# A decoder layer in seven-product matmuls: which quads take seven products where the left operand is new, when its sums are made, and the queues of the first loads

## The chip, the cores and the metric

The kernel runs on 1 core of a Trainium2 chip. The metric is the device time of one execution in microseconds (us); lower is better. The engines are PE (TensorE, matmuls), DVE (VectorE), ACT (ScalarE), POOL (GpSimd) and SP (SyncE, which here only issues DMAs). All inputs lie in HBM.

## The reference, cut to what matters

One layer on x of 256 tokens by 4096 features, in float32:

```python
def reference(x, norm_gain, w_in, conv_w, w_out, rel_bias, final_gain):
    ...
    u = rmsnorm(h, norm_gain[l])
    proj = jnp.einsum('bsd,df->bsf', u, w_in[l])          # 4096 -> 16384
    q, k, v, z_a, hc, b_gate, c_gate, z_c = jnp.split(proj, split_at, axis=-1)
    ...
    attn = moba_attention(q, k, v, rel_bias).reshape(B, S, ATTN_W) * jax.nn.silu(z_a)
    conv = b_gate * short_conv(c_gate * hc, conv_w[l]) * jax.nn.silu(z_c)
    mixed = jnp.concatenate([attn, conv], axis=-1)
    h = h + jnp.einsum('bsf,fd->bsd', mixed, w_out[l])    # 4096 -> 4096
    return rmsnorm(h, final_gain)
```

With 256 tokens there is one attention block, so attention is causal softmax over 256 positions with a bias by distance, for 16 heads of 128. The convolution has three taps. Nearly all the work is in the two projections.

## The kernel before

**Parts.** A float32 product is made of three matmuls. Each operand is split into hi (rounded to the fast type, on ACT) and lo (the rest, on DVE), and hi x hi, lo x hi and hi x lo are added up in PSUM (L533 to L535). A matmul takes a 128 x 128 block of the left operand as weights and 512 columns of the right one.

**Pairs and quads.** A pair `p` is two column blocks of 512 over all 4096 rows: 16 pairs of the input projection (0 to 15, ordered by `PAIRS`) and 4 of the output projection (16 to 19). A pair has 16 quads, each for one `q`: 256 rows of the contraction, so 2 token halves x 2 row blocks on the left and 2 x 2 blocks on the right. The list `ORDERS` says in which order a pair takes its quads; places are counted from 0. `load` fetches the 1 MB of weights of a quad (`raw`, three buffers), two quads ahead.

**Eight or seven products.** Written out, a quad is eight block products, 24 matmuls, into four PSUM banks (3, 8, 2, 4). A quad of the set `SEVEN` (q = 0, 2, 4, 6, 8, 10, 12) takes seven, 21 matmuls, by sums of blocks on both sides: DVE makes four sums of weight blocks (`sum`, L465 to L467) and splits seven blocks of them in place of four; the left operand needs sums too (`sums_of`, L112, four subtractions or additions of 128 columns, then `parts` on seven blocks). The products go to banks 1, 5, 6, 7 besides. I call such quads sevens and the others eights. When the last seven of a pair is through, `early` (or `out_early` in the output) reads banks 1, 5, 6 and 7 into four tiles `e` on DVE, and ACT scales them by the tokens' norm (L587); when the pair is through, `two_done` (or `out_end`) reads banks 3, 2, 4, 8 on DVE and adds them (late sums). In between `tasks_of` puts the attention or the convolution of an earlier pair, counted by block products after the last seven (`behind`).

**What sets the order.** A unit is one split of hi and lo: an eight has two, a seven three. `split` runs two units ahead of the matmuls, and hi and lo have a ring of three buffers, so ACT and DVE can be two units ahead of PE at most. The engines take their instructions in the order in which the scheduler has put them; an instruction that waits holds back those behind it on its engine. All DMAs stand in SP's queue in order.

**Where the left operand is new.** In pair 0 the x blocks are loaded quad by quad (`x_load`, 256 KB), scaled by the norm's gain and split (`x_parts`): for an eight straight into hi (L138) and lo (L139), for a seven by way of a tile `c` (L130), its sums (L114) and `parts` (L117, L118). The tiles `k` are kept for all 16 pairs. The sums of squares of x are made by ACT on eight further loads of 512 KB (`squares`). In pairs 15 and 16 the same is done with the mixed rows (`m_load` from a DRAM tile `m_d`, then `m_parts`), at the places in `M_AT`. Pair 0 takes the order `FIRST` and pair 16 `OUT_FIRST`, both with eights between sevens; the last seven stands at place 14 of pair 0, 13 of pair 16 and 12 of all others. All pairs have the same seven sevens.

**Start and end.** Eight matmuls on zeros (`WARM`) run ahead of the first quad. The first loads are x, the gains and the weights, all from SP. In the last pair the products of the last three units for banks 3 and 2 (the second token half) are kept back, `out_end` and `finish` of the first half are written ahead of them, and then the kept products run unit by unit, bank 3 and bank 2 in turn.

## Time and profile before

| | us |
|---|---|
| median of 3 runs | 1749.53 (1748.86 to 1749.96) |
| the profiled execution, whole | 1750.47 |
| its span, first to last instruction | 1748.4 |
| PE busy | 1715.6 |
| DVE busy | 1533.4 |
| ACT busy | 1035.3 |

The span is 2.1 us short of the execution's own time. Busy time of PE is the union of overlapping records: a matmul's record lasts about 0.39 us, while the next one starts 0.23 us after it, so a stage is judged by how many matmuls it got through. A window row gives, for each engine, busy us and the number of instructions that lie in it (x...), then the granted TensorE clock as a share of 2.4 GHz, the share of DMA time and GB/s. A record on a window's edge is counted on both sides.

### The profile page before, as it was taken

To read this page: it belongs to the slowest core of one execution; us is meant where nothing else is said; L and a number is where in the kernel's file an instruction comes from. 1 tells how busy PE (TensorE), PEld (TensorE's weight loads), DVE (VectorE), ACT (ScalarE), POOL (GpSimd) and SP (SyncE) were. 2 spreads that over 40 slices of the span, in tenths; PEclk is the share of its full clock that TensorE was granted. 3 is DMA by queue.
4 is the path that set the end of the run, shared out by engine and by line. 5 is a ranking of instruction groups with operands and counts; after the bars stand their busy time and mean duration, and the time that the engine had idled before them with its cause. 6 is when DMAs were issued, how large, how long until landed. Compare 5 with 4: busy or idle time off the path is not lost.

```text
span 1748.4 us, 20772 instructions
## 1 busy us (share of the span) xinstructions
PE 1715.6 (98%) x7638; PEld 1402.8 (80%) x7638; DVE 1533.4 (88%) x1678; ACT 1035.3 (59%) x1125; POOL 0.7 (0%) x6
## 2 busy tenths in 40 slices
...
GB/s 298 310 169 215 187 216 200 198 187 216 203 195 187 217 204 193 192 203 197 213 198 212 205 211 198 199 210 218 203 205 223 233 282 239 200 207 208 200 220 154
DMA packets 65265, 368.18 MB, mean 211 GB/s; under 512 B 8811, under 2 KB 13452, under 8 KB 24460
## 3 DMA queue, kind: packets, MB, share of 16 engines
...
HBM read 357.66 MB, written 9.18 MB: 210 GB/s over the span
## 4 chain that ended last, share of the span: by engine, by line
PE 90%; DVE 7%; issue 1%; ACT 1%; DMA 0%; SPq 0%; DVEq 0%; ACTq 0%
PE p L535 29%; PE p L533 29%; PE p L534 29%; DVE lo L477 3%; ACT hi L476 1%; DVE sum L465 1%; DVE sum L466 1%; DVE k L118 0%; DVE sum L467 0%; PE p L220 0%; PE p L227 0%; DVE c L114 0%; PE p L244 0%; DVE hg L400 0%; DVE hg L406 0%
## 5 line engine op out<-in xcount | busy, mean ns | idle before, releaser
L533 PE MATMUL p<-hi,k 128*128 128x512 f32 x2420 | 949.5, 394 | 14.0 <-ACT hi L476 11.3
L534 PE MATMUL p<-hi,k 128*128 128x512 f32 x2420 | 945.2, 391 | 0.5 <-DVE k L118 0.3
L535 PE MATMUL p<-lo,k 128*128 128x512 f32 x2420 | 930.8, 392 | 2.5 <-DVE lo L477 2.3
L477 DVE TENSOR_TENSOR lo<-raw,hi 128x1024 fp32r<-128x1024 f32 (+2 forms) x504 | 675.9, 1359 | 42.4 <-ACT hi L476 41.2
L476 ACT CAST hi<-raw 128x1024 fp32r<-128x1024 f32 (+2 forms) x504 | 581.6, 1165 | 209.0 <-PE p L534 173.1
L476 ACT CAST hi<-sum 128x1024 fp32r<-128x1024 f32 x280 | 295.0, 1053 | 444.5 <-PE p L534 244.8
L533 PEld LDWEIGHTS p<-hi,k 128*128 128x128 f32 x2420 | 455.1, 188 | 115.4 <-ACT hi L476 19.2
L535 PEld LDWEIGHTS p<-lo,k 128*128 128x128 f32 x2420 | 455.0, 188 | 106.9 <-DVE lo L477 10.0
L534 PEld LDWEIGHTS p<-hi,k 128*128 128x128 f32 x2420 | 456.4, 189 | 93.9 <-DVE k L118 3.1
L477 DVE TENSOR_TENSOR lo<-sum,hi 128x1024 fp32r<-128x1024 f32 x280 | 341.9, 1221 | 135.3 <-ACT hi L476 135.1
L465 DVE TENSOR_TENSOR sum<-raw 128x1024 f32<-128x1024 f32 x140 | 170.9, 1221 | 8.6 <-DMA raw<-in_w_dram 6.3
L467 DVE TENSOR_TENSOR sum<-sum,raw 128x512 f32<-128x512 f32 x140 | 95.9, 685 | 0.2
L466 DVE TENSOR_TENSOR sum<-sum,raw 128x512 f32<-128x512 f32 x140 | 95.8, 684 | 0.2
L587 ACT ACTIVATE e<-e,rT 128x512 f32<-128x512 f32 x56 | 37.8, 716 | 0.7 <-DVE e L320 0.7
L117 ACT CAST k<-c 128x896 fp32r<-128x896 f32 (+1 forms) x23 | 18.7, 813 | 9.8 <-PE p L535 7.7
L118 DVE TENSOR_TENSOR k<-c,k 128x896 fp32r<-128x896 f32 (+1 forms) x23 | 21.2, 927 | 1.5 <-ACT k L117 1.5
L258 DVE SCALAR_TENSOR_TENSOR am<-p,st,z 128x128 f32<-128x128 f32 x32 | 9.7, 344 | 7.5 <-PE p L255 7.5
L305 DVE SCALAR_TENSOR_TENSOR y<-p,cw,y 128x255 f32<-128x255 f32 (+1 forms) x32 | 15.2, 477 | 0.1
L114 DVE TENSOR_TENSOR c<-c 128x128 f32<-128x128 f32 x56 | 14.3, 282 | 0.1
L235 ACT ACTIVATE lg<-lg,st 128x256 f32<-128x256 f32 (+1 forms) x32 | 14.3, 447 | 0.0
L303 ACT ACTIVATE y<-p,cw 128x256 f32<-128x256 f32 x16 | 7.6, 473 | 11.2 <-PE p L301 11.2
L402 ACT ACTIVATE e<-hg 128x512 f32<-128x512 f32 x16 | 10.0, 625 | 6.9 <-DVE hg L400 6.6
...
## 6 DMA issues: line engine op xcount, KB each, us to landing
raw<-in_w_dram SPq DMA_DIRECT2D x254, 1024.0 KB, 4.8
raw<-in_wout_dram SPq DMA_DIRECT2D x64, 1024.0 KB, 4.8
...
hg<-in_xres_dram SPq DMA_DIRECT2D x4, 1024.0 KB, 9.5
...
```

The costliest lines, as they stand in the source:

```text
L117: nc.scalar.copy(dst[:, :, 0], c)
L118: nc.vector.tensor_tensor(dst[:, :, 1], c, dst[:, :, 0].bitcast(F32), ALU.subtract)
L305: nc.vector.scalar_tensor_tensor(y[:, i:], ps[:, :S - i], cw[:, k, 2 - i:3 - i], y[:, i:], op0=ALU.mult, op1=ALU.add)
L465: nc.vector.tensor_tensor(t[:, :2], raw[:, 1:3], raw[:, :1].to_broadcast([P, 2, B]), ALU.add)
L466: nc.vector.tensor_tensor(t[:, 2], t[:, 0], raw[:, 2], ALU.add)
L467: nc.vector.tensor_tensor(t[:, 3], t[:, 2], raw[:, 3], ALU.add)
L476: nc.scalar.copy(hi[:, c], src[:, c])
L477: nc.vector.tensor_tensor(lo[:, c], src[:, c], hi[:, c].bitcast(F32), ALU.subtract)
L533: nc.tensor.matmul(acc[b_], a, h_, start=s0, stop=False)
L534: nc.tensor.matmul(acc[b_], b, h_, start=False, stop=False)
L535: nc.tensor.matmul(acc[b_], a, l_, start=False, stop=s1)
L587: nc.scalar.activation(es[name], es[name], AF.Copy, scale=rows[c][:, t:t + 1])
```

## The change

- Pair 0 and pair 16 now have three sevens (q = 8, 10, 12) and 13 eights; pair 1 has five sevens (4 to 12 even). The set of sevens is kept for each pair (`SEVENS`). Both pairs take one new order `FIRST`, with the sevens at places 9, 11 and 13.
- The missing sums of q = 0, 2, 4, 6 are made later (`made_up`): the x blocks are loaded again and scaled in pair 1 after places 1 (q = 4), 3 (6), 12 (0) and 14 (2); the mixed rows are loaded again in pair 16 after places 6, 8, 10 and 12 (`RAISE`). The load is written one place ahead. The sum that stood in slot 7 of a left operand now replaces the block in slot 0.
- `M_AT` is a table, the operands of the mixed rows being spread over 16 places of pairs 15 and 16.
- The four scalings after `early` are put behind 5, 8, 11 and 14 block products, in all pairs of the input projection.
- The gains and the first x are loaded from ACT's queue, the first weights from SP's. There are 12 warm-up matmuls.
- At the end, the kept products of bank 3 all run ahead of those of bank 2, and `out_end` of bank 3 is written between them.

The diff:

```diff
--- before.py
+++ after.py
@@ -28,7 +28,7 @@
 QUAD = 4 * B
-WARM = 8
+WARM = 12
 AHEAD = 2
@@ -47,14 +47,24 @@
 SEVEN = frozenset((0, 2, 4, 6, 8, 10, 12))
-FIRST = (1, 3, 0, 5, 2, 7, 4, 9, 6, 11, 8, 13, 10, 14, 12, 15)
+FIRST = (1, 3, 5, 7, 0, 9, 2, 11, 4, 8, 6, 10, 13, 12, 14, 15)
 USUAL = (0, 1, 2, 3, 4, 5, 6, 7, 8, 9, 10, 11, 12, 13, 14, 15)
-OUT_FIRST = (1, 3, 5, 0, 7, 2, 9, 4, 11, 6, 13, 8, 12, 10, 14, 15)
 N_PAIRS = 16
...
 PAIRS += [x for g in range(4) for x in (((4, 6), g), ((7, 5), g))]
-ORDERS = [FIRST] + [USUAL] * (N_PAIRS - 1) + [OUT_FIRST] + [USUAL] * (NDP - 1)
+ORDERS = [FIRST] + [USUAL] * (N_PAIRS - 1) + [FIRST] + [USUAL] * (NDP - 1)
+SEVENS = [SEVEN] * (N_PAIRS + NDP)
+SEVENS[0] = SEVENS[N_PAIRS] = SEVEN - {0, 2, 4, 6}
+SEVENS[1] = SEVEN - {0, 2}
+RAISE = {(1, 1): 4, (1, 3): 6, (1, 12): 0, (1, 14): 2,
+         (N_PAIRS, 6): 0, (N_PAIRS, 8): 2, (N_PAIRS, 10): 4, (N_PAIRS, 12): 6}
+M_AT = {(15, 3): 1, (15, 5): 3, (15, 7): 5, (15, 8): 7, (15, 9): 0, (15, 10): 9, (15, 11): 2,
+        (15, 13): 11, (15, 14): 4, (15, 15): 8, (16, 0): 6, (16, 2): 10, (16, 3): 13, (16, 5): 12,
+        (16, 7): 14, (16, 9): 15}
@@ -103,34 +113,37 @@
     def operands(q):
-        n = 7 if q in SEVEN else 4
-        A[q] = kt.tile([P, n, 2, P], F32R, name=f"k{q}")
+        A[q] = kt.tile([P, 7 if q in SEVEN else 4, 2, P], F32R, name=f"k{q}")
         return A[q]
...
-        for dst, a, b, op in ((4, 0, 2, ALU.subtract), (7, 1, 0, ALU.subtract),
-                              (5, 4, 1, ALU.subtract), (6, 3, 5, ALU.add)):
+        for dst, a, b, op in ((4, 0, 2, ALU.subtract), (5, 4, 1, ALU.subtract),
+                              (6, 3, 5, ALU.add), (0, 1, 0, ALU.subtract)):
             nc.vector.tensor_tensor(c[:, dst], c[:, a], c[:, b], op)
...
-    def x_load(q, place):
+    def x_load(q):
         xr = pool.tile([P, 2, S], F32, name="xr", tag="pt", bufs=4)
-        nc.sync.dma_start(xr, xT[place].rearrange("p (k t) -> p k t", k=2))
+        nc.sync.dma_start(xr, xT[q].rearrange("p (k t) -> p k t", k=2))
         return xr
+    def x_scaled(q, xr):
+        c = ep.tile([P, 8, P], F32, name="c", bufs=2)
+        for j in range(2):
+            nc.scalar.activation(c[:, 2 * j:2 * j + 2], xr[:, j].rearrange("p (a b) -> p a b", a=2),
+                                 AF.Copy, scale=g_sb[:, 2 * q + j:2 * q + j + 1])
+        return c
...
         dst = operands(q)
-        if q in SEVEN:
-            c = ep.tile([P, 8, P], F32, name="c", bufs=2)
-            for j in range(2):
-                nc.scalar.activation(c[:, 2 * j:2 * j + 2], xr[:, j].rearrange("p (a b) -> p a b", a=2),
-                                     AF.Copy, scale=g_sb[:, 2 * q + j:2 * q + j + 1])
+        if q in SEVENS[0]:
+            c = x_scaled(q, xr)
             sums_of(c)
-            parts(dst, c[:, 1:])
+            parts(dst, c[:, :7])
             return
@@ -146,11 +159,16 @@
         dst = operands(q)
-        if q in SEVEN:
+        if q in SEVENS[N_PAIRS]:
             sums_of(c)
-            parts(dst, c[:, 1:])
+            parts(dst, c[:, :7])
         else:
-            parts(dst, c[:, :4])
+            parts(dst[:, :4], c[:, :4])
+    def made_up(q, c):
+        sums_of(c)
+        parts(A[q][:, 4:], c[:, 4:7])
+        parts(A[q][:, :1], c[:, :1])
@@ -326,6 +344,9 @@
+    def scaled(e, r):
+        nc.scalar.activation(e, e, AF.Copy, scale=r)
     def two_done(dsts, rows):
@@ -392,9 +413,9 @@
-    def out_end(p, ts=(1, 0)):
+    def out_end(p, ts=(1, 0), accs=(2, 3, 4, 8)):
         for b_, t, n, _ in ENDS:
-            if t not in ts:
+            if t not in ts or b_ not in accs:
                 continue
@@ -429,9 +450,12 @@
         if p == 0:
-            xrs[q] = x_load(q, i)
             if i == 0:
-                nc.sync.dma_start(g_sb, gain)
+                nc.scalar.dma_start(g_sb, gain)
+                xr = xrs[q] = pool.tile([P, 2, S], F32, name="xr", tag="pt", bufs=4)
+                nc.scalar.dma_start(xr, xT[q].rearrange("p (k t) -> p k t", k=2))
+            else:
+                xrs[q] = x_load(q)
         if n < LEAD:
@@ -440,11 +464,11 @@
     def units_of(n):
-        q = quads[n][2]
-        if q in SEVEN:
-            return [(n, "raw", 1, ((((0, 1),)), ((5, 3),), ((2, 2),))),
-                    (n, "sum", 0, (((3, 5),), ((6, 7),))),
-                    (n, "sum", 2, (((4, 6),), ((1, 4),)))]
+        p, _, q = quads[n]
+        if q in SEVENS[p]:
+            return [(n, "raw", 1, (((1, 1),), ((6, 3),), ((3, 2),))),
+                    (n, "sum", 0, (((4, 5),), ((0, 7),))),
+                    (n, "sum", 2, (((5, 6),), ((2, 4),)))]
         return [(n, "raw", 0, (((1, 3), (0, 8)), ((1, 2), (0, 4)))),
@@ -459,7 +483,7 @@
                 x_parts(q, xrs.pop(q))
-            if q in SEVEN:
+            if q in SEVENS[p]:
                 raw = raws[n].rearrange("p (b c) -> p b c", b=4)
@@ -501,12 +525,7 @@
               + [x for g in range(4) for x in ((hc_end, g), (zb_end, g))])
-    M_AT = {}
-    for j, q in enumerate(OUT_FIRST):
-        at = (15, (3, 5, 7, 8, 9, 10, 11, 12, 13, 14, 15)[j]) if j < 11 else (16, (0, 1, 2, 5, 6)[j - 11])
-        M_AT[at] = q
-    m_order = [OUT_FIRST[j] for j in range(NQ)]
+    m_order = list(M_AT.values())
     m_raw = {}
@@ -514,7 +533,7 @@
     split(1)
-    last_seven = [max(i for i, q in enumerate(o) if q in SEVEN) for o in ORDERS]
+    last_seven = [max(i for i, q in enumerate(o) if q in SEVENS[p]) for p, o in enumerate(ORDERS)]
     plan = {}
@@ -534,7 +553,7 @@
-    behind, tasks, kept = None, {}, []
+    behind, tasks, kept, raised = None, {}, [], {}
     for u, (n, kind, at, products) in enumerate(units):
@@ -583,17 +602,24 @@
                 rows = (rQ if p < 8 and p % 2 == 0 else rT, rT)
-                for _, t, c, name in ENDS:
-                    nc.scalar.activation(es[name], es[name], AF.Copy, scale=rows[c][:, t:t + 1])
+                for j, (_, t, c, name) in enumerate(ENDS):
+                    tasks.setdefault(5 + 3 * j, []).append((scaled, (es[name], rows[c][:, t:t + 1])))
             else:
...
             at = m_order.pop(0)
+            assert at == M_AT[p, i]
             m_parts(at, m_raw.pop(at))
...
                 m_raw[m_order[0]] = m_load(m_order[0])
+        if (p, i + 1) in RAISE:
+            q = RAISE[p, i + 1]
+            raised[q] = x_load(q) if p < N_PAIRS else m_load(q)
+        if (p, i) in RAISE:
+            q = RAISE[p, i]
+            made_up(q, x_scaled(q, raised.pop(q)) if p < N_PAIRS else raised.pop(q))
         if i == NQ - 1:
@@ -603,12 +629,13 @@
     finish(0)
-    for u, hi, lo, products in kept:
-        for b0, pr in enumerate(products):
-            for a_, b_ in pr:
-                if b_ in (3, 2):
-                    block(u, hi, lo, b0, a_, b_)
-    out_end(NDP - 1, (1,))
+    for acc_ in (3, 2):
+        for u, hi, lo, products in kept:
+            for b0, pr in enumerate(products):
+                for a_, b_ in pr:
+                    if b_ == acc_:
+                        block(u, hi, lo, b0, a_, b_)
+        out_end(NDP - 1, (1,), (acc_,))
     finish(1)
@@ -637,7 +664,7 @@
     return {
-        "xT": x[0].T.reshape(NQ, 2, P, S).transpose(0, 2, 1, 3).reshape(NQ, P, 2 * S)[list(FIRST)],
+        "xT": x[0].T.reshape(NQ, 2, P, S).transpose(0, 2, 1, 3).reshape(NQ, P, 2 * S),
         "xres": x[0].reshape(2, P, NDP, 2 * B).transpose(2, 1, 0, 3).reshape(NDP, P, 4 * B),
```

The engine orders at three places, taken from the built programs, each before and after. Numbers behind names tell buffers apart; `k0` is the left operand of q = 0.

DVE in pair 0, from the third quad on, before (L114 and L118 make x sums, L465 to L467 weight sums, L477 lo parts, L139 lo of an eight's x):

```order
L114 TENSOR_TENSOR c_201<-c_201 128x128 x4
L118 TENSOR_TENSOR k0_200<-c_201,k0_200 128x7x128
L465 TENSOR_TENSOR sum_210<-raw_117 128x1024
L477 TENSOR_TENSOR lo_215<-raw_117,hi_214 128x1536
L466 TENSOR_TENSOR sum_210<-sum_210,raw_117 128x512
L477 TENSOR_TENSOR lo_231<-sum_210,hi_230 128x1024
L467 TENSOR_TENSOR sum_210<-sum_210,raw_117 128x512
L139 SCALAR_TENSOR_TENSOR k5_264<-xr_139,g_sb_63,k5_264 128x2x128
L194 COPY row_194<-p5_192 16x384
L139 SCALAR_TENSOR_TENSOR k5_264<-xr_139,g_sb_63,k5_264 128x2x128
L477 TENSOR_TENSOR lo_247<-sum_210,hi_246 128x1024
```

DVE at the same place after (L501 makes lo parts, L152 lo of an eight's x, L212 copies a bias row):

```order
L152 SCALAR_TENSOR_TENSOR k5_204<-xr_122,g_sb_63,k5_204 128x2x128 x2
L501 TENSOR_TENSOR lo_210<-raw_121,hi_209 128x1024
L501 TENSOR_TENSOR lo_226<-raw_121,hi_225 128x1024
L152 SCALAR_TENSOR_TENSOR k7_245<-xr_143,g_sb_63,k7_245 128x2x128 x2
L501 TENSOR_TENSOR lo_251<-raw_142,hi_250 128x1024
L212 COPY row_198<-p5_196 16x384
L501 TENSOR_TENSOR lo_267<-raw_142,hi_266 128x1024
L152 SCALAR_TENSOR_TENSOR k0_286<-xr_201,g_sb_63,k0_286 128x2x128 x2
L501 TENSOR_TENSOR lo_292<-raw_200,hi_291 128x1024
L152 SCALAR_TENSOR_TENSOR k9_327<-xr_242,g_sb_63,k9_327 128x2x128 x2
L501 TENSOR_TENSOR lo_308<-raw_200,hi_307 128x1024
```

The third quad was a seven with four x sums, a copy of seven blocks and four weight sums; now quads 3 to 5 are eights with two lo parts and two x parts each.

PE at the step from pair 0 (k15) to pair 1 (k0), before (names p1 to p8 are banks):

```order
L535 MATMUL p2_161<-lo_867,k15_851 128x512
L533 MATMUL p4_165<-hi_866,k15_851 128x512
L534 MATMUL p4_165<-hi_866,k15_851 128x512
L535 MATMUL p4_165<-lo_867,k15_851 128x512
L533 MATMUL p1_937<-hi_895,k0_200 128x512
L534 MATMUL p1_937<-hi_895,k0_200 128x512
L535 MATMUL p1_937<-lo_896,k0_200 128x512
L533 MATMUL p5_955<-hi_911,k0_200 128x512
L534 MATMUL p5_955<-hi_911,k0_200 128x512
L533 MATMUL p3_941<-hi_895,k0_200 128x512
L534 MATMUL p3_941<-hi_895,k0_200 128x512
L535 MATMUL p3_941<-lo_896,k0_200 128x512
```

PE at the same step after:

```order
L554 MATMUL p2_165<-lo_834,k15_812 128x512
L552 MATMUL p4_169<-hi_833,k15_812 128x512
L553 MATMUL p4_169<-hi_833,k15_812 128x512
L554 MATMUL p4_169<-lo_834,k15_812 128x512
L552 MATMUL p3_899<-hi_853,k0_286 128x512
L553 MATMUL p3_899<-hi_853,k0_286 128x512
L554 MATMUL p3_899<-lo_854,k0_286 128x512
L552 MATMUL p3_899<-hi_870,k0_286 128x512
L552 MATMUL p2_907<-hi_853,k0_286 128x512
L553 MATMUL p2_907<-hi_853,k0_286 128x512
L554 MATMUL p2_907<-lo_854,k0_286 128x512
L552 MATMUL p4_911<-hi_853,k0_286 128x512
```

Before, pair 1 starts on banks 1 and 5; now it starts on banks 3 and 2, which the late sums of pair 0 read, and its first quad is an eight.

DVE in pair 1 around q = 4, before (the raw and sum rows are those of one seven and of the eight after it):

```order
L465 TENSOR_TENSOR sum_1052<-raw_976 128x1024
L477 TENSOR_TENSOR lo_1057<-raw_976,hi_1056 128x1536
L466 TENSOR_TENSOR sum_1052<-sum_1052,raw_976 128x512
L477 TENSOR_TENSOR lo_1073<-sum_1052,hi_1072 128x1024
L467 TENSOR_TENSOR sum_1052<-sum_1052,raw_976 128x512
L477 TENSOR_TENSOR lo_1089<-sum_1052,hi_1088 128x1024
L477 TENSOR_TENSOR lo_1104<-raw_1028,hi_1103 128x1024
L477 TENSOR_TENSOR lo_1114<-raw_1028,hi_1113 128x1024
```

DVE around q = 4 of pair 1 after (L123 makes left sums, L127 their lo parts, L489 to L491 weight sums):

```order
L123 TENSOR_TENSOR c_968<-c_968 128x128 x4
L501 TENSOR_TENSOR lo_982<-raw_893,hi_981 128x1024
L127 TENSOR_TENSOR k4_459<-c_968,k4_459 128x3x128
L127 TENSOR_TENSOR k4_459<-c_968,k4_459 128x128
L489 TENSOR_TENSOR sum_1017<-raw_934 128x1024
L501 TENSOR_TENSOR lo_998<-raw_893,hi_997 128x1024
L490 TENSOR_TENSOR sum_1017<-sum_1017,raw_934 128x512
L491 TENSOR_TENSOR sum_1017<-sum_1017,raw_934 128x512
L501 TENSOR_TENSOR lo_1022<-raw_934,hi_1021 128x1536
L123 TENSOR_TENSOR c_1053<-c_1053 128x128 x3
L501 TENSOR_TENSOR lo_1038<-sum_1017,hi_1037 128x1024
L123 TENSOR_TENSOR c_1053<-c_1053 128x128
```

The sums of q = 4 now stand ahead of its weight sums, and those of q = 6 between its lo parts.

## Rows read from the trace of the kernel before

**Rows 1.** The page's first part, PE's and PE loads' busy time, with DVE, ACT and POOL.

```profile
PE 1715.6 (98%) x7638; PEld 1402.8 (80%) x7638; DVE 1533.4 (88%) x1678; ACT 1035.3 (59%) x1125; POOL 0.7 (0%) x6
```

**Rows 2.** The waits of PE from 200 to 1390 us: the heading of the answer, under which no row stands.

```profile
engine line waited for: us in total, times, longest us
```

**Rows 3.** Windows by pair: pair 0, pair 10 (with 16 transposes of the convolution), pair 11 (no other task), pair 16 (with 16 transposes), pair 17.

```profile
6.40:108.50 102.10, 94.05 (x365) 71.22 (x366) 95.03 (x135) 75.53 (x104) 0.00 (x0) 0.93 0.78 278
...
889.60:973.90 84.30, 84.30 (x381) 69.66 (x380) 75.62 (x82) 49.39 (x50) 0.00 (x0) 1.00 0.57 206
...
973.90:1056.30 82.40, 82.40 (x364) 67.88 (x363) 72.20 (x71) 46.14 (x44) 0.00 (x0) 1.00 0.58 205
...
1390.00:1481.50 91.50, 87.50 (x380) 68.50 (x380) 85.63 (x104) 50.16 (x50) 0.00 (x0) 1.00 0.71 260
1481.50:1567.70 86.20, 83.60 (x364) 67.59 (x363) 78.36 (x81) 48.44 (x52) 0.00 (x0) 1.00 0.58 204
```

**Rows 4.** Windows inside pair 0: its start, its middle, its end, and a stretch of the middle.

```profile
6.40:24.00 17.60, 17.35 (x66) 13.18 (x67) 15.40 (x24) 12.19 (x18) 0.00 (x0) 0.90 0.92 343
24.00:88.00 64.00, 61.49 (x258) 47.01 (x257) 63.27 (x91) 54.85 (x77) 0.00 (x0) 1.00 0.87 309
88.00:108.50 20.50, 15.21 (x44) 11.03 (x43) 16.35 (x22) 8.49 (x10) 0.00 (x0) 0.75 0.38 125
20.00:80.00 60.00, 58.62 (x243) 43.97 (x242) 59.94 (x82) 50.76 (x71) 0.00 (x0) 1.00 0.85 309
```

**Rows 5.** The timeline at the end of pair 0: start, us, engine, line, instruction, idle time before it and its releaser.

```profile
94.53 0.69 DVE L318 TENSOR_TENSOR e<-p,e 128x512 f32<-128x512 f32 x1 [1.27 <-PE p L535]
...
95.31 0.72 ACT L587 ACTIVATE e<-e,rQ 128x512 f32<-128x512 f32 x1 [3.31 <-DVE e L318]
...
98.56 3.35 ACT L476 CAST hi<-raw 128x1024 fp32r<-128x1024 f32 x3
...
99.64 0.79 PE L533 MATMUL p<-hi,k 128*128 128x512 f32 x1 [4.92 <-ACT hi L476]
...
101.49 0.63 PE L533 MATMUL p<-hi,k 128*128 128x512 f32 x1
```

**Rows 6.** The two slow stretches of pairs 16 and 17 as windows, and one wait of ACT in the first (timeline).

```profile
1457.00:1470.00 13.00, 10.28 (x39) 6.31 (x37) 11.21 (x12) 6.46 (x8) 0.00 (x0) 1.00 0.30 98
1482.00:1500.00 18.00, 15.40 (x64) 11.26 (x63) 16.83 (x21) 11.80 (x18) 0.00 (x0) 1.00 0.49 161
...
1460.34 1.04 ACT L476 CAST hi<-sum 128x1024 fp32r<-128x1024 f32 x1 [2.94 <-DVE sum L467]
```

**Rows 7.** The timeline of the tail: DVE and the last matmul.

```profile
1733.33 0.39 PE L535 MATMUL p<-lo,k 128*128 128x512 f32 x1
...
1733.83 2.20 DVE L418 TENSOR_SCALAR hg<-hg,rf 128x512 f32<-128x512 f32 x4
...
1736.55 0.68 DVE L400 TENSOR_TENSOR hg<-p,hg 128x512 f32<-128x512 f32 x1
```

**Rows 8.** DVE's groups by line and form from 20 to 80 us: count, busy us, mean ns of one, idle before.

```profile
L477 DVE TENSOR_TENSOR lo<-raw,hi 128x1024 fp32r<-128x1024 f32 x10 | 11.7, 1211 | 0.0
L477 DVE TENSOR_TENSOR lo<-raw,hi 128x1536 fp32r<-128x1536 f32 x5 | 8.7, 1743 | 0.0
L465 DVE TENSOR_TENSOR sum<-raw 128x1024 f32<-128x1024 f32 x5 | 6.0, 1210 | 0.0
L139 DVE SCALAR_TENSOR_TENSOR k<-xr,g_sb,k 128x256 fp32r<-128x256 f32 x12 | 5.6, 471 | 0.0
L118 DVE TENSOR_TENSOR k<-c,k 128x896 fp32r<-128x896 f32 x5 | 5.4, 1076 | 0.0
L114 DVE TENSOR_TENSOR c<-c 128x128 f32<-128x128 f32 x20 | 4.9, 276 | 0.0
L466 DVE TENSOR_TENSOR sum<-sum,raw 128x512 f32<-128x512 f32 x6 | 4.1, 679 | 0.0
```

**Rows 9.** The step from pair 15 to pair 16: the last of the four late reads (timeline) and the window around it.

```profile
1392.34 0.74 DVE L332 SCALAR_TENSOR_TENSOR b<-p,rT,e 128x512 f32<-128x512 f32 x1
...
1390.00:1400.00 10.00, 10.00 (x49) 8.06 (x49) 10.00 (x17) 6.06 (x8) 0.00 (x0) 1.00 0.64 225
```

**Rows 10.** The timeline of the first 10 us: DMA issues (SPq), the warm-up, the first scaling, cast and matmuls.

```profile
0.74 0.39 SPq L122 DMA_DIRECT2D xr<-in_xT_dram  x1
...
1.19 3.21 PE L97 MATMUL p<-zero 128*128 128x512 bf16 x8 [1.19 <-DVE tab L187]
...
1.65 1.85 SPq L437 DMA_DIRECT2D raw<-in_w_dram  x4
...
3.68 0.91 ACT L138 ACTIVATE k<-xr,g_sb 128x256 fp32r<-128x256 f32 x2 [1.47 <-DMA g_sb<-in_gain_dram]
...
5.78 1.38 ACT L476 CAST hi<-raw 128x512 fp32r<-128x512 f32 x2 [1.19 <-DMA raw<-in_w_dram]
...
6.45 0.50 PE L533 MATMUL p<-hi,k 128*128 128x512 f32 x1 [2.05 <-ACT hi L476]
...
8.49 0.63 PE L533 MATMUL p<-hi,k 128*128 128x512 f32 x1
...
8.91 0.63 PE L534 MATMUL p<-hi,k 128*128 128x512 f32 x1
```

**Rows 11.** The page's sixth part, weight loads: count, KB of one, median us from issue to landing.

```profile
raw<-in_w_dram SPq DMA_DIRECT2D x254, 1024.0 KB, 4.8
```

## The prediction

> **What bounds the kernel now.** I read the engine table first: PE is busy 1715.6 of 1748.4 us [rows 1], but matmul records overlap, so that figure hides slow stretches. I therefore went to the waits of PE in the long middle, from 200 to 1390 us: the list is empty [rows 2]. There a pair takes what its matmuls take: 364 records in 82.40 us in pair 11, so 0.2264 us each, and 381 in 84.30 us in pair 10, which has 16 short transposes besides [rows 3]. That pace is the floor, and nothing in the middle can be won except by fewer matmuls. What is lost stands at three places, each found by laying a stage's time beside its matmuls at this pace.
>
> Pair 0: 365 records in 102.1 us, 19.4 us over the floor. Its three stretches [rows 4] say where. From 6.4 to 24 us, 66 matmuls (14.95 us) took 17.6: 2.65 lost, at a granted clock of 0.90. From 24 to 88 us, 258 (58.4 us) took 64.0: 5.6 lost, with DVE busy 63.27 us of it. From 88 to 108.5 us, 44 (10.0 us) took 20.5: 10.5 lost, at a clock of 0.75. In the last one PE stands 4.92 us until 99.64: ACT's queue held four scalings of the early sums (95.31 to about 98.6), the first behind a 3.31 us wait on DVE, ahead of the next hi casts [rows 5]. After such gaps the clock is at its lower level, 1.2 GHz: a matmul lasts 0.63 us there [rows 5].
>
> Pair 16: 380 records in 91.50 us against 84.30 in pair 10: 7.3 lost. Pair 17: 86.20 against 82.40: 3.8 lost [rows 3]. The places are 1457 to 1470 us, three quads of seven products in a row, and 1482 to 1500, where DVE does the early and the late sums of the output next to each other [rows 6].
>
> The tail: the last matmul starts at 1733.33, but bank 2, the last to be read, is only taken up by DVE at 1736.55, behind the scaling of the other token half [rows 7].
>
> **The change part by part.** The sum is made against the profiled execution, 1750.47 us, which is 0.94 over the median of the runs, 1749.53.
>
> *Matmuls.* Four quads of pair 0, four of pair 16 and two of pair 1 go from seven to eight products: 10 products of three matmuls, 30 x 0.2264 = **6.8 us lost** on PE, which ends everywhere last. This is certain.
>
> *The load taken off DVE in pair 0.* In the mean durations of [rows 8], a seven costs DVE 1.21 + 2 x 0.68 for the weight sums, 1.74 + 2 x 1.21 for the lo parts, 4 x 0.276 + 1.08 for the x sums and their lo: 8.9 us. An eight costs 2 x 1.21 + 2 x 0.47 = 3.4. One of each is 12.3 by the durations; they overlap a little, and the stretch 20 to 80 us shows the true pace: 243 matmuls in 60 us [rows 4], so 45 of them, a seven and an eight, in 11.1. PE needs 45 x 0.2264 = 10.2. So DVE is the bound by 0.9 us for each two quads. Now pair 0 has 3 sevens and 13 eights: (3 x 8.9 + 13 x 3.4) x 11.1/12.3 = 64 us of DVE against 375 x 0.2264 = 84.9 us of PE. The nine eights at the start let DVE run ahead until the ring of three hi/lo buffers is full. The three sevens at places 9, 11 and 13 are then again each 0.9 us short with their eight, 2.3 us in all, and the lead covers part of it. Of the middle's 5.6 us I take **4.6 back**; bounds 2.5 (the lead helps nothing and the token scale's chain adds to it) and 5.6.
>
> *The hole at the end of pair 0.* The four scalings leave ACT's queue as one block; they are now put after 5, 8, 11 and 14 block products, and the last seven stands one place earlier (13 in place of 14), so two quads, 48 matmuls or 10.9 us, lie over the 4 x 0.69 us of early sums [rows 5]. The hi casts of those quads stand ahead of the scalings. What is late next is the first quad of pair 1. It is an eight now and starts on bank 3, which the late sums still have to read (before, it started on bank 1, free since the early sums). The same step stands in the trace at 1390: DVE gives the last bank free at about 1393.1, and PE loses nothing in 1390 to 1400, 49 matmuls with 10.00 us busy [rows 9]. Without that cover it would be the four late reads of 0.74 us, about 3 us. Of 10.5 us I take **10.0 back**; bounds 7.5 and 10.5.
>
> *The start.* The first weights were issued at 1.65 us, behind x and the gains; the first hi cast waited for them until 5.78, the first matmul came at 6.45 [rows 10]. They are now issued at about 0.74, and x and the gains go through ACT, where they stand ahead of the table load; ACT had 1.47 us idle before its first scaling, so that costs nothing, but would cost up to 0.9 us if its casts became late. I take a start at 5.4: **1.05 gained**; bounds 0.3 (the 12 warm-up matmuls end last, with four more at the lower clock's 0.43 each after 4.40) and 1.3. The Trainium skill, "DMA: Bandwidth & Descriptors", section "Issuing engines are not separate DMA queues", speaks against more: DMAs issued from several engines share the same 16 engines and interleave, and only issue time is saved. By it x and the first weights hold each other up, the term is at most the 0.91 us of issue, and the sum would be 0.15 to 0.9 us smaller; no run so far shows the two queues side by side. The longer warm-up also closes the gap from 4.40 to 6.45, after which the matmuls at 8.49 ran at 0.43 apart, the lower level [rows 10]. Of the 2.65 us lost there I take **2.1 back** (DVE must still make the lo part of x between the first and the second matmul); bounds 0.5 and 2.65.
>
> *Sums made later.* A quad's missing parts cost DVE four subtractions of 0.276 and a lo part in two pieces, 384 and 128 columns. The trace has no 384; between 128 (0.276) and 896 (1.08) a straight line gives 0.54, so 1.9 us a quad. The Trainium skill, "VectorE: DVE Perf Modes", section on the trn2 errata, gives (N + 151)/0.96 ns for this kind of operation, 557 ns for 384; the term is the same by it. In pair 1 the two quads that became eights take 2 x 4.3 us off DVE (6.7 without x parts against 2.4) and the four made-up quads put 7.7 on, so the total hardly moves, but they stand between the sevens 4 and 6, and 8 to 12, where DVE has little spare: in pair 11, with no other task, it is busy 72.20 of 82.40 us [rows 3]. I take **1.0 lost**; bounds 0 and 3. In pair 16 they stand among the sevens at places 9, 11 and 13.
>
> *Pair 16.* The sevens alternate with eights in place of three in a row, and the first half has none, so that the conv and the operands fit. Of 7.3 us I take **6.1 back**; bounds 4.0 (the made-up sums of two quads, 3.8 us, are not covered) and 7.3. The step into pair 17 has the same work on DVE in the same order, so of its 3.8 us only **0.3**; bounds -1.0 and 2.5.
>
> *The tail.* Bank 3 is now finished nine matmuls before bank 2, and DVE takes bank 2 at about 1733.8, 2.7 us earlier. But its gain product still stands behind the scaling of the other half, and that scaling starts later, because the squares of bank 3 are now ahead of its root on ACT. The output DMAs of that half move back by an estimated 1.4 us and then run into those of the second. I take **0.3**; bounds -0.3 and 2.2.
>
> *The scalings in the other pairs.* Their cover is the empty list of [rows 2]: 0. Uncovered, they would stand on ACT as before.
>
> *Sum:* 4.6 + 10.0 + 1.05 + 2.1 - 6.8 - 1.0 + 6.1 + 0.3 + 0.3 = 16.65 us. 1750.47 - 16.65 = 1733.8, and by the median 1732.9. **I predict 1733 us.** All bounds at their low ends would leave a gain of 3 us, all at their high ends 25.
>
> **The rivals.** *The sevens stay late.* The made-up sums and the x sums meet the sevens in pairs 0, 1 and 16 and use up DVE's lead, and new waits bring the clock down again. For it: 11.1 against 10.2 us per seven and eight; ACT, at 50.76 of 60 us [rows 4], has little room too. Against it: nine eights ahead of them. With the middle of pair 0, pair 1 and pair 16 at their low bounds, 2.1 + 2.0 + 2.1 = 6.2 us less: 1739 us, 1737 to 1745.
>
> *All waits go.* The low-cost ends at the end of pair 0, pair 1, pair 16 and half of pair 17: 1.0 + 0.5 + 1.0 + 1.2 + 1.5 = 5.2 more: 1728 us, down to 1725. For it: DVE's 64 us in a stage of 85. Against it: the sevens stand close together, and the step into pair 17 isn't changed.
>
> *Slower: weights behind the made-up loads.* The x and mixed rows for the later sums are loaded again through SP, in whose queue the 1 MB weight loads stand behind them. If such a load waits for its buffer (the two `c` tiles, read by DVE late), the weights wait too. A weight load is asked for about two quads, 10.9 us, before use and takes 4.8 to land [rows 11], so a wait under 6 us costs nothing, and from there each us costs one. With the eight loads waiting a seven and an eight long, 11 us, it would be 8 x 5 = 40 us: 1773. It decides from 2.1 us of excess for each of the eight. Against it: the buffers are then used by these loads and few others.
>
> *The gains and the price cancel:* all terms near their low bounds, 1746 to 1750.
>
> **How the numbers follow.** Forecast (1728 to 1738) 0.57; sevens stay late 0.23; all waits go 0.12; slower 0.04; cancelled 0.04. The range 1727 to 1742 leaves out the slower cases, the end of the first rival and some of the second. A measurement of this kernel tells about 0.2%, 3.5 us, from no change: faster 0.92, the same 0.04, slower 0.04.
>
> **What would show it.** Right: pair 1's first matmul near 95 us in place of 108; no clock under 0.95 in any stretch after the start; PE's waits in pair 0 under 3 us and none on ACT's scalings; pair 16 near 88 us; pair 17 near 86. Wrong: DVE at 10 of 10 us in places 9 to 13 with PE waiting there (first rival); weight sums waiting on DMA (slower); the first matmul after 6 us (start). The sum falls if the step from pair 0 to pair 1 holds PE for its bank and the clock drops with it.

## The result, and the profile after

The kernel after takes 1733.46 us (median, 1732.80 to 1735.79) against 1749.27 for the kernel before on the same chip (1748.86 to 1749.96): a ratio of 0.9912, 95% interval 0.9894 to 0.9929. The forecast was 1733. The profiled execution took 1733.7 us, its span is 1731.9, so 16.5 us less than the span of before.

The page's first part answers to [rows 1]: PE has 34 instructions more (30 matmuls and 4 of the warm-up) and is busy 3.5 us less all the same, since slow matmuls and short waits under overlapping records had counted as busy before; DVE has lost 35 us.

```profile
PE 1712.1 (99%) x7672; PEld 1407.2 (81%) x7672; DVE 1498.0 (86%) x1658; ACT 1026.2 (59%) x1135; POOL 0.7 (0%) x6
```

PE's waits from 0 to 200 us, by releaser: us in total, times, longest. Before, this stretch held the hole of 4.92 us of [rows 5]; now the longest is the one ahead of the warm-up. From 200 to 1370 us the list is empty, as in [rows 2].

```profile
PE p L107 <- DVE tab L205: 1.2, 1, 1.2
PE p L552 <- ACT k L151: 0.9, 1, 0.9
PE p L554 <- DVE lo L501: 0.5, 1, 0.5
```

Windows by pair: pair 0, pair 1, pairs 15, 16 and 17. They answer to [rows 3] (same columns).

```profile
7.30:94.90 87.60, 87.03 (x378) 70.34 (x379) 72.39 (x105) 66.42 (x98) 0.00 (x0) 1.00 0.87 314
94.90:184.90 90.00, 90.00 (x415) 74.24 (x414) 77.17 (x105) 58.77 (x84) 0.00 (x0) 1.00 0.58 201
1295.20:1378.90 83.70, 83.61 (x372) 68.63 (x371) 79.78 (x89) 54.90 (x58) 0.00 (x0) 1.00 0.67 237
1378.90:1465.70 86.80, 86.52 (x384) 71.15 (x385) 72.95 (x101) 45.52 (x51) 0.00 (x0) 1.00 0.74 279
1465.70:1551.00 85.30, 83.70 (x365) 67.65 (x364) 77.31 (x80) 48.29 (x53) 0.00 (x0) 1.00 0.58 207
```

Pair 0 lasts 87.6 us in place of 102.1, at a granted clock of 1.00 in place of 0.93, with DVE busy 72.39 us in place of 95.03. Pair 16 lasts 86.8 in place of 91.5, and pair 15, which now has 8 of the 16 convolution transposes, 83.7 in place of 82.7 (a window of before from 1307.3 to 1390.0).

The end of pair 0 on ACT answers to [rows 5]: the hi casts (L500) and the four scalings (L348) take turns: casts stand ahead of the scalings and between them.

```profile
84.45 1.04 ACT L500 CAST hi<-raw 128x1024 fp32r<-128x1024 f32 x1
86.70 0.73 ACT L348 ACTIVATE e<-e,rQ 128x512 f32<-128x512 f32 x1 [1.21 <-DVE rQ L197]
87.33 1.03 ACT L500 CAST hi<-raw 128x1024 fp32r<-128x1024 f32 x1
88.27 0.72 ACT L348 ACTIVATE e<-e,rT 128x512 f32<-128x512 f32 x1
88.89 0.71 ACT L348 ACTIVATE e<-e,rQ 128x512 f32<-128x512 f32 x1
89.50 1.04 ACT L500 CAST hi<-raw 128x1024 fp32r<-128x1024 f32 x1
```

The start answers to [rows 10], and it went the wrong way: x, issued at 1.17 from ACT's queue (ACTq), is there at 6.76, after the first weights and after the warm-up's end, and the first matmul comes at 7.32, not 5.4 (and not 6.45, as before).

```profile
0.73 1.81 SPq L461 DMA_DIRECT2D raw<-in_w_dram  x4
...
1.17 0.46 ACTq L456 DMA_DIRECT2D xr<-in_xT_dram  x1
...
1.19 5.26 PE L107 MATMUL p<-zero 128*128 128x512 bf16 x12 [1.19 <-DVE tab L205]
...
4.56 0.62 ACT L500 CAST hi<-raw 128x512 fp32r<-128x512 f32 x1 [1.42 <-DMA raw<-in_w_dram]
...
6.76 0.91 ACT L151 ACTIVATE k<-xr,g_sb 128x256 fp32r<-128x256 f32 x2 [1.58 <-DMA xr<-in_xT_dram]
...
7.32 0.50 PE L552 MATMUL p<-hi,k 128*128 128x512 f32 x1 [0.87 <-ACT k L151]
```

The tail answers to [rows 7]. Bank 2 is read (L421) 0.72 us after the last matmul's start, not 3.2. But the first half's scaling (L439) starts 2.07 us after it, not 0.5, and with it the output DMAs (SPq).

```profile
1716.45 0.39 PE L554 MATMUL p<-lo,k 128*128 128x512 f32 x1
...
1717.17 0.67 DVE L421 TENSOR_TENSOR hg<-p,hg 128x512 f32<-128x512 f32 x1
...
1718.52 2.21 DVE L439 TENSOR_SCALAR hg<-hg,rf 128x512 f32<-128x512 f32 x4
...
1719.04 8.19 SPq L440 DMA_DIRECT2D out_dram<-hg  x10
```

From the start of the last matmul to the end of the span it is 15.45 us (1731.9 - 1716.45), against 15.07 before (1748.4 - 1733.33).

### The profile page after: what moved, and what is told of

It reads as the page before. It is cut to its first block, busy times and chain, and to the rows that moved or that the text cites. A ratio compares the mean times of both kernels' runs of the same rounds, so it can differ in the third digit from the quotient of the medians.

```text
span 1731.9 us, 20846 instructions
## 1 busy us (share of the span) xinstructions
PE 1712.1 (99%) x7672; PEld 1407.2 (81%) x7672; DVE 1498.0 (86%) x1658; ACT 1026.2 (59%) x1135; POOL 0.7 (0%) x6
## 4 chain that ended last, share of the span: by engine, by line
PE 95%; DVE 2%; issue 1%; DMA 1%; ACT 1%; ACTq 0%; DVEq 0%; SPq 0%
PE p L554 31%; PE p L552 31%; PE p L553 31%; DVE lo L501 1%; DMA c<-m_d 0%; ACT hi L500 0%; PE p L238 0%; PE p L245 0%; DMA xr<-in_xT_dram 0%; PE p L262 0%; DVE hg L439 0%; DVE sum L489 0%; PE p L273 0%; PE p L271 0%; PE p L272 0%
## 5 line engine op out<-in xcount | busy, mean ns | idle before, releaser
L501 DVE TENSOR_TENSOR lo<-raw,hi 128x1024 fp32r<-128x1024 f32 (+2 forms) x514 | 683.9, 1347 | 64.3 <-ACT hi L500 63.2
L500 ACT CAST hi<-raw 128x1024 fp32r<-128x1024 f32 (+2 forms) x514 | 589.1, 1154 | 249.6 <-PE p L553 211.6
L500 ACT CAST hi<-sum 128x1024 fp32r<-128x1024 f32 x260 | 273.9, 1054 | 402.3 <-PE p L553 246.9
L501 DVE TENSOR_TENSOR lo<-sum,hi 128x1024 fp32r<-128x1024 f32 x260 | 317.8, 1222 | 128.4 <-ACT hi L500 128.2
L489 DVE TENSOR_TENSOR sum<-raw 128x1024 f32<-128x1024 f32 x130 | 158.9, 1222 | 12.2 <-DMA raw<-in_w_dram 8.7
L491 DVE TENSOR_TENSOR sum<-sum,raw 128x512 f32<-128x512 f32 x130 | 89.3, 687 | 0.3
L490 DVE TENSOR_TENSOR sum<-sum,raw 128x512 f32<-128x512 f32 x130 | 89.2, 686 | 0.1
L348 ACT ACTIVATE e<-e,rT 128x512 f32<-128x512 f32 x56 | 38.3, 718 | 0.0
L126 ACT CAST k<-c 128x512 fp32r<-128x512 f32 (+3 forms) x35 | 19.6, 576 | 13.2 <-PE p L554 6.0
L127 DVE TENSOR_TENSOR k<-c,k 128x512 fp32r<-128x512 f32 (+3 forms) x35 | 21.8, 635 | 0.8 <-ACT k L126 0.8
L123 DVE TENSOR_TENSOR c<-c 128x128 f32<-128x128 f32 x56 | 14.1, 287 | 2.6 <-ACT c L137 1.2
```

Of the source, the lines that this page charges most:

```text
L126: nc.scalar.copy(dst[:, :, 0], c)
L127: nc.vector.tensor_tensor(dst[:, :, 1], c, dst[:, :, 0].bitcast(F32), ALU.subtract)
L348: nc.scalar.activation(e, e, AF.Copy, scale=r)
L489: nc.vector.tensor_tensor(t[:, :2], raw[:, 1:3], raw[:, :1].to_broadcast([P, 2, B]), ALU.add)
L490: nc.vector.tensor_tensor(t[:, 2], t[:, 0], raw[:, 2], ALU.add)
L491: nc.vector.tensor_tensor(t[:, 3], t[:, 2], raw[:, 3], ALU.add)
```

## The experiments

One execution of each kernel was profiled. Beside the experiments the kernel before took 1748.95 to 1749.74 us (medians), so medians that lie less than 1 us apart are not told apart here.

For pair 0 a table is easier to read than rows. It gives the start of four main matmuls in us, counted on PE's timeline: the first, the 67th, the 331st and the first of pair 1. Pair 0 has 363 of them in before, e2, e5, e10 and e11, 369 in e12 and 375 in the others.

| kernel | 1st | 67th | 331st | pair 1 |
|---|---|---|---|---|
| before | 6.45 | 24.61 | 92.37 | 108.52 |
| after | 7.32 | 23.70 | 84.44 | 94.86 |
| e1, scalings in a block | 7.28 | 23.65 | 84.39 | 94.82 |
| e2, old sevens | 7.12 | 25.49 | 91.56 | 107.80 |
| e5, before + spread | 6.25 | 24.85 | 91.19 | 107.65 |
| e9, last seven at 14 | 7.62 | 25.61 | 85.46 | 96.34 |
| e10, before, last at 13 | 6.36 | 24.81 | 101.77 | 109.25 |
| e11, before, POOL sums | 6.33 | 25.89 | 97.46 | 105.65 |
| e7, old pair 16 | 7.33 | 25.11 | 85.84 | 96.30 |
| e8, sums three times | 7.87 | 24.23 | 84.96 | 95.39 |
| e4, old tail | 7.79 | 25.34 | 86.22 | 96.65 |
| e3, x first on SP | 5.66 | 22.68 | 84.69 | 94.90 |
| e6, 8 warm-ups | 7.37 | 24.97 | 86.96 | 97.18 |
| e12, five sevens | 8.04 | 26.47 | 87.75 | 96.58 |

**The scalings back in a block.**

```diff
-                    tasks.setdefault(5 + 3 * j, []).append((scaled, (es[name], rows[c][:, t:t + 1])))
+                    scaled(es[name], rows[c][:, t:t + 1])
```

> The kernel after, with the four scalings of the early sums again in one block on ACT in all pairs. If the block of scalings makes the hole at the end of pair 0 (theory): PE waits there again on a hi cast of L500 and the clock falls with it; the last seven now stands one place earlier, so I expect 4 to 8 us lost, 1738 to 1741 us, pair 0 lasting 92 to 96 us in place of 87.5, and nothing lost in pairs 1 to 15, whose DVE and ACT are ahead. If the sevens of pair 0 alone made it (rival), the place of the scalings no longer matters with nine eights ahead: 1733 to 1734 us and no wait of PE over 1 us before 200 us.

Measured: 1732.99 us (1732.84 to 1734.66), the time of after. The theory falls. Three scalings stand in a row on ACT now, with no cast between them, and PE loses nothing, since the casts it needs had been made:

```profile
88.21 0.71 ACT L348 ACTIVATE e<-e,rT 128x512 f32<-128x512 f32 x1
88.83 0.71 ACT L348 ACTIVATE e<-e,rQ 128x512 f32<-128x512 f32 x1
89.44 0.71 ACT L348 ACTIVATE e<-e,rT 128x512 f32<-128x512 f32 x1
```

**The old sevens in the kernel after.** `FIRST` and `OUT_FIRST` as before, `RAISE = {}`, and

```diff
-SEVENS[0] = SEVENS[N_PAIRS] = SEVEN - {0, 2, 4, 6}
-SEVENS[1] = SEVEN - {0, 2}
```

> The kernel after with the products and orders of the kernel before in pairs 0, 1 and 16 (7638 matmuls in place of 7668 in the main work, no sums made later); the scalings stay spread, in pair 0 after 1, 3, 5 and 7 block products, as only one quad is left there; start, warm-up and end as after. If the fewer sevens earn the middle of pair 0 and pair 16 (theory): 4.6 and 6.1 come back as losses and some 2 us of the hole, against 6.8 of matmuls saved: about 6 us more than after, 1737 to 1741 us. If the spread scalings do most of it (rival), the time falls by the matmuls, to 1727 to 1731 us, below both kernels.

Measured: 1748.96 us (1747.72 to 1751.09), ratio to before 0.9998 (0.9990 to 1.0007). So all that the change gives is in its sevens, with the orders, the sums made later and the places of the mixed rows' operands that go with them; spread, start, warm-up and tail together give nothing beside the old sevens. The loss is over twice what I expected because the hole is back whole: pair 1 starts at 107.80, and ACT again has the four scalings, from 94.83, ahead of three hi casts, from 98.07.

**The spread alone, in the kernel before.** The four scalings as tasks after 1, 3, 5 and 7 block products in pair 0, after 5, 8, 11 and 14 elsewhere.

> The kernel before with the four scalings spread alone (in pair 0 after 1, 3, 5 and 7 block products, elsewhere after 5, 8, 11 and 14). Theory: only the hole at the end of pair 0 shrinks, 6 to 10 us: 1739 to 1743 us, with DVE busy nearly all of 20 to 80 us as before and pairs 16 and 17 at 91.5 and 86.2 us. Rival, that the scalings hold up the lo parts and with them the whole of pair 0 and pair 16: 1733 us or less.

Measured: 1748.34 us (1747.07 to 1750.81), ratio 0.9992 (0.9983 to 1.0001). Both theories are wrong: the hole is untouched. PE's waits from 0 to 200 us, and ACT at the end of pair 0:

```profile
PE p L536 <- ACT hi L479: 6.4, 2, 4.9
...
94.52 0.72 ACT L330 ACTIVATE e<-e,rQ 128x512 f32<-128x512 f32 x1 [2.75 <-DVE e L318]
...
97.14 0.71 ACT L330 ACTIVATE e<-e,rT 128x512 f32<-128x512 f32 x1
97.76 3.35 ACT L479 CAST hi<-raw 128x1024 fp32r<-128x1024 f32 x3
```

Though the code puts the scalings between the products of the last quad, the built program still has all four ahead of the next three hi casts. The scheduler set the order, not the line in the code. By what it chooses the order no run shows.

**The last seven back at place 14, with three sevens.** `ORDERS[0]` ends on 13, 14, 12, 15, and the scalings come after 1, 3, 5 and 7 products in pair 0.

> The kernel after with the last seven of pair 0 at place 14 again (places 12 and 14 of its order changed about, still three sevens; scalings after 1, 3, 5 and 7 block products, as one quad is left). The first runs showed that the spread of the scalings does nothing, so the theory is now that the hole was DVE's and ACT's lack of lead under seven sevens: with three, the hi casts of the last quad still stand ahead of the scalings and the hole does not come back: 1733 to 1735 us, pair 0 at 87.5 to 89 us, no wait of PE over 2 us there. Rival, that the quad of cover more behind the last seven closed it: 4 to 8 us lost, 1737 to 1741 us.

**The last seven at place 13, with seven sevens**, in the kernel before:

```diff
-FIRST = (1, 3, 0, 5, 2, 7, 4, 9, 6, 11, 8, 13, 10, 14, 12, 15)
+FIRST = (1, 3, 0, 5, 2, 4, 7, 6, 9, 8, 11, 10, 13, 12, 14, 15)
```

> The kernel before with pair 0's order changed alone: all seven sevens, the last at place 13 (places 2, 4, 5, 7, 9, 11, 13), so two quads of eight behind it. Theory, the lead: DVE is as late as before and the hole at the end of pair 0 stays: 1747 to 1751 us, a wait of PE of 3 to 5 us on a hi cast near 93 us. Rival, the cover of one quad more: the hole shrinks by 5 to 10 us: 1739 to 1745 us.

Measured: e9 1733.12 us (1732.24 to 1734.70); e10 1752.72 (1751.46 to 1753.48). Both speak for the lead and against the place, though e10 lies 1.7 us above the range of its theory. In e9 only one quad stands behind the last seven, and PE's longest wait there is 0.5 us; in e10 there are two, and it waits 6.0 us, where 3 to 5 were expected. In e10 ACT too has the four scalings ahead of three hi casts. The waits of PE from 0 to 200 us, first of e9, then of e10, and ACT at the end of pair 0 in e10:

```profile
PE p L553 <- ACT k L152: 1.7, 1, 1.7
...
PE p L553 <- DVE k L354: 0.5, 1, 0.5
```

```profile
PE p L533 <- ACT hi L476: 7.6, 2, 6.0
...
92.37 0.72 ACT L587 ACTIVATE e<-e,rQ 128x512 f32<-128x512 f32 x1 [3.02 <-DVE rQ L179]
...
94.83 2.92 ACT L476 CAST hi<-raw 128x1024 fp32r<-128x1024 f32 x3
```

**The left sums on POOL, in the kernel before:**

```diff
-            nc.vector.tensor_tensor(c[:, dst], c[:, a], c[:, b], op)
+            nc.gpsimd.tensor_tensor(c[:, dst], c[:, a], c[:, b], op)
```

> The kernel before with the four sums of a seven's left operand made by POOL in place of DVE, in pair 0 and for the mixed rows; all products and orders as before (7638 matmuls). Theory, DVE's load in pair 0 makes both the slow middle and the hole: each seven there gives up 4 x 0.276 = 1.1 us of DVE, a seven and an eight then cost DVE 10.0 us against 10.2 of PE, so most of the 16 us of middle and hole and part of pair 16's 7.3 come back without a product more: 1733 to 1740 us, if POOL's sums take DVE no time. Rival, ACT or the weight sums are the bound: 1747 us or more.

Measured: 1759.87 us (1758.47 to 1761.68), slower than before. A sum takes 977 ns on POOL against 276 on DVE [rows 8]; ACT's casts of the sums then wait for POOL (12.2 us in all between 20 and 100 us), and pair 15, where POOL makes the sums of the mixed rows, becomes 9.9 us longer. So the run cannot say what DVE's load costs in the middle. At the end of pair 0 three casts stand ahead of the scalings, as in after, and from 88 to 110 us PE gets 86 matmuls done at a clock of 1.00 [rows 4: 44 in 20.5 us at 0.75], with seven sevens and the last at 14. From the 331st to pair 1's first, 33 matmuls, it takes 8.19 us where before takes 16.15 (table), so seven sevens alone do not make the hole. As PE had lost time to POOL earlier in the pair, the run does not say what DVE's relief has to do with it. POOL's sums by form over the whole run, ACT's wait, that window, and ACT in it:

```profile
L114 POOL TENSOR_TENSOR c<-c 128x128 f32<-128x128 f32 x56 | 53.9, 977 | 1347.4 <-DMA c<-m_d 1284.3 <-ACT c L130 61.4
...
ACT k L117 <- POOL c L114: 12.2, 4, 3.4
...
88.00:110.00 22.00, 20.03 (x86) 15.56 (x85) 21.15 (x31) 17.34 (x22) 0.00 (x0) 1.00 0.67 198
...
98.53 3.38 ACT L476 CAST hi<-raw 128x1024 fp32r<-128x1024 f32 x3
102.79 0.73 ACT L587 ACTIVATE e<-e,rQ 128x512 f32<-128x512 f32 x1 [0.89 <-DVE e L318]
```

**Pair 16 as before, in the kernel after.** Its order, its seven sevens and `M_AT` as before, no made-up sums there:

```diff
-SEVENS[0] = SEVENS[N_PAIRS] = SEVEN - {0, 2, 4, 6}
+SEVENS[0] = SEVEN - {0, 2, 4, 6}
```

> The kernel after with pair 16's order, its seven sevens and the places of the mixed rows' operands as before (12 matmuls fewer, 2.7 us). Theory, the three sevens in a row and the operands' sums make pair 16 slow: 6.1 to 6.4 us lost against 2.7 saved, 1736 to 1738 us, pairs 15 and 16 together at about 174 us in place of 170.5. Rival, the slow stretch of pair 16 comes from what pair 0 left behind or from DMA: then it does not come back and the time falls to 1730.5 to 1731.5 us.

Measured: 1739.80 us (1738.35 to 1739.97). Windows of pairs 15, 16 and 17, and the waits of PE from 1370 to 1570 us:

```profile
1296.40:1379.20 82.80, 82.80 (x365) 67.67 (x364) 79.41 (x93) 52.79 (x56) 0.00 (x0) 1.00 0.63 231
1379.20:1470.90 91.70, 87.45 (x381) 68.53 (x380) 85.70 (x104) 49.85 (x50) 0.00 (x0) 1.00 0.70 259
1470.90:1557.10 86.20, 83.56 (x365) 67.63 (x364) 78.32 (x81) 48.44 (x52) 0.00 (x0) 1.00 0.57 205
```

```profile
PE p L553 <- ACT hi L501: 4.8, 6, 1.0
PE p L555 <- DVE lo L502: 1.9, 3, 1.1
```

The three pairs take 260.7 us against 255.8 in after, though they have 12 matmuls (2.7 us) fewer: pair 16's change earns 7.6 and pays 2.7, and 0.9 of it comes in pair 17. The slow stretch hung on nothing that pair 0 left behind. The run takes pair 16's order, its sevens, its made-up sums and the places in `M_AT` back together, so it does not tell what each is worth. The time is 1.8 us above the theory's range; 1.4 us of the difference stand at the start (table, 67th).

**The made-up sums split three times over.** In `made_up`, a loop of three around the two `parts`.

> The kernel after with the split of the made-up sums written three times over (the same values again), 2 x 0.8 us of DVE and as much of ACT more for each of the four quads of pair 1 and the four of pair 16. Theory, the made-up sums lie in DVE's slack and cost nothing: in pair 1 still nothing, at most 1 us a quad among the sevens of pair 16; 1733 to 1737 us. Rival, they stand on DVE's limit, as the prediction's 1.0 us for pair 1 has it: 8 x 1.6 = 13 us, 1745 us or more.

Measured: 1734.75 us (1734.03 to 1734.84), 1.3 more than after, 0.5 of it at the start (table); pair 17, from its first matmul to pair 18's, is 1.3 us longer, too. Pair 1 holds 5 us more of DVE's work and takes 0.1 us longer (its window; in after 90.00 with DVE at 77.17); pair 16 is no longer than in after.

```profile
95.30:185.40 90.10, 90.10 (x415) 74.23 (x414) 82.13 (x121) 63.06 (x99) 0.00 (x0) 1.00 0.59 202
```

**x first on SP's queue, the gains on ACT's**, in the kernel after:

```diff
-                xr = xrs[q] = pool.tile([P, 2, S], F32, name="xr", tag="pt", bufs=4)
-                nc.scalar.dma_start(xr, xT[q].rearrange("p (k t) -> p k t", k=2))
+                xrs[q] = x_load(q)
```

> The kernel after with the first x at the head of SP's queue, ahead of the weights, and the gains on ACT's. Theory: x lands before the weights and the first matmul follows the last warm-up at 6.45 us in place of 7.32: 0.9 us gained, 1732.6 us. Rival, the order in which they are issued makes no difference, since both share the engines: the first matmul at 7.1 us or later, 1733.5 us.

Measured: 1733.32 us (1732.73 to 1733.47), the time of after, and yet the start is better by more than either theory said: x is used 2.95 us after its issue, not 5.59, and what ACT waited for last was the gains; the first matmul starts at 5.66.

```profile
0.74 0.39 SPq L131 DMA_DIRECT2D xr<-in_xT_dram  x1
...
3.69 0.91 ACT L151 ACTIVATE k<-xr,g_sb 128x256 fp32r<-128x256 f32 x2 [1.04 <-DMA g_sb<-in_gain_dram]
...
5.66 0.53 PE L551 MATMUL p<-hi,k 128*128 128x512 f32 x1
```

At the 67th matmul 1.0 us of the 1.7 is left, and that goes near 82 us: the built program has ACT scale both x blocks of the quad (L151) ahead of a cast there, where after has the cast first, and PE waits 1.3 us for a cast, which after does not have. The same order and the same wait stand in e6. So an edit of the start came with a change of order elsewhere that has nothing to do with it.

**Eight warm-up matmuls**, `WARM = 8` in the kernel after.

> The kernel after with 8 warm-up matmuls in place of 12. Theory: the four more keep the clock up; without them PE stands from 4.6 to 7.3 us, the clock falls as in the kernel before, and matmuls run at the lower level for some 4 us: 1.5 to 2.1 us lost, 1735 to 1735.6 us, with a granted clock under 0.95 in the first 20 us. Rival, the clock at the start hangs on the first quads' waits and not on the warm-up: 1733 to 1734 us.

Measured: 1736.16 us (1735.01 to 1737.08), 2.7 more than after. At the 67th matmul 1.27 us are lost, the rest is the wait near 82 us. PE waits 2.58 us after the warm-up and then runs about seven matmuls 0.43 apart, records of 0.63, the level of [rows 10], though the clock column from 7.3 to 10.5 us shows 1.00 (in e4, which follows, it shows 0.52). But e4, with 12 warm-ups and x landing late, shows the same, and so does e7, in which x comes no later than in after (PE's timeline of e6, of e4, and of e7 with its warm-up):

```profile
7.37 1.22 PE L552 MATMUL p<-hi,k 128*128 128x512 f32 x2 [2.58 <-ACT k L151]
8.38 0.63 PE L553 MATMUL p<-hi,k 128*128 128x512 f32 x1
```

```profile
7.79 0.80 PE L552 MATMUL p<-hi,k 128*128 128x512 f32 x1 [2.46 <-ACT k L151]
...
8.90 0.63 PE L554 MATMUL p<-lo,k 128*128 128x512 f32 x1
```

```profile
1.19 4.16 PE L108 MATMUL p<-zero 128*128 128x512 bf16 x12 [1.19 <-DVE tab L206]
...
7.33 0.70 PE L553 MATMUL p<-hi,k 128*128 128x512 f32 x1 [1.99 <-ACT k L152]
```

In after all twelve warm-up matmuls stand 0.43 us apart and end at 6.45; in e7 and e4 the last ones stand 0.21 apart, the higher level, so the same twelve end at 5.35, PE then stands idle for 1.99 and 2.46 us, and the clock falls. Six kernels here start with the same lines (after, e1, e4, e7, e8, e9); their 67th matmul lies between 23.65 and 25.61, 24.61 in the mean, which is the kernel before's time. In the three in which PE stood 0.8 to 1.4 us between the warm-up and the first matmul (after, e1, e8) none of the first 66 matmuls stand 0.43 apart, and the 67th comes at 23.65 to 24.23; in the three in which it stood 1.67 to 2.46 us (e9, e7, e4) some do, and it comes at 25.11 to 25.61. So the four matmuls more did not keep the clock in every execution, and what they are worth is not shown: e6's 67th, at 24.97, lies within the spread of the six.

**The end as before**, in the kernel after: the kept products unit by unit and one `out_end`.

> The kernel after with the end of the kernel before: the kept products unit by unit, bank 3 and bank 2 in turn, one read of both behind them. Theory: the output of the other half is waiting for its scaling and DMAs, so it is no slower: from the start of the last matmul to the end 15.1 us in place of 15.45, 1733.1 us. Rival, bank 2 taken up 2.7 us sooner is worth what it says: 1735.5 to 1736 us without it.

Measured: 1734.34 us (1732.44 to 1735.12). From the last matmul's start to the end it is 15.08 us in place of 15.45, so the theory holds for the tail; the start took it back (67th matmul 1.64 later). In the sum it can't be seen.

**Five sevens in pair 0**, further apart, all seven in pair 1, and the old end:

```diff
+FIRST5 = (1, 3, 4, 5, 7, 6, 9, 0, 8, 11, 2, 10, 13, 12, 14, 15)
+SECOND = (4, 1, 6, 3, 8, 5, 0, 7, 2, 9, 10, 11, 12, 13, 14, 15)
...
-SEVENS[1] = SEVEN - {0, 2}
+SEVENS[0] = SEVEN - {0, 2}
```

> The kernel after with five sevens in pair 0 in place of three, at places 2, 5, 8, 11 and 13, so nearly always two quads of eight between two of them; pair 1 takes all seven sevens (in the order 4, 1, 6, 3, 8, 5, 0, 7, 2, 9 to 15), with only q = 0 and 2 made up, after places 1 and 3; and the end of the kernel before. 12 matmuls fewer than after. Theory, DVE is short only where a seven has a single eight beside it: a seven and two eights cost DVE 15.7 us of instructions, 14.2 at the overlap seen, against 15.7 of PE, so pair 0 stays free of waits and the time falls by 12 x 0.2264 + 0.4 = 3.1 us, to 1730.3 us. Rival, any further seven in pair 0 brings its waits back, 0.9 us or more for each and the hole with them: 1732 to 1740 us.

Measured: 1735.93 us (1735.28 to 1737.06), 2.5 more than after: by the total the rival wins, but not by its mechanism. From the 67th to the 331st matmul, 264 in both, pair 0 takes 61.28 us against 60.74, and up to pair 1 it saves 1.05 of the 1.36 us that six matmuls are worth. So five spaced sevens cost pair 0 hardly anything behind its start, as the theory had it. What was lost lies at the start (67th matmul 2.77 us later: x lands late, and the third quad is a seven again) and in pair 1, 91.1 us against 90.0 with six matmuls fewer. There PE waits for DVE three times, 1.4 us in all, before 115 us; that the sums of q = 0 and 2 meet sevens there is the likely reason, and no run tests it.

## Why the prediction was right, step by step

The time was right to half a microsecond, and in part that is luck: the start came 2.25 us short and the tail 0.7, and pair 0 (0.9), the sums made later (1.0) and pairs 16 and 17 (0.9) made up for it. The reason given for the largest term named the wrong lever.

- *Matmuls*, -6.8: each of the three lines has 2430 instructions in place of 2420, and their pace is as before. As put.
- *Middle and hole of pair 0*, 4.6 + 10.0: between the 67th matmul and pair 1's first, before takes 83.91 us and after 71.16 with 12 more, so 12.75 + 2.72 = 15.5 against 14.6. The size is right. For the middle the step was DVE's load, and the traces agree: from the 67th to the 331st matmul DVE is busy 65.77 of 66.08 us in e2 (seven sevens), 57.87 of 61.28 in e12 (five) and 49.90 of 60.74 in after (three), ACT 55.02, 52.55 and 48.26. (Three sevens short by 0.9 us each make 2.7, not the 2.3 of the working; and the low ends of all bounds leave 3.7 us, not 3.) For the hole the step that failed is "the four scalings leave ACT's queue as one block; they are now put after 5, 8, 11 and 14 block products, and the last seven stands one place earlier": e1 (block, no hole), e5 (spread in the code, hole), e10 (two quads behind, hole) and e9 (one quad, no hole) show that neither closes the hole beside seven sevens and neither is needed beside three; both undone at once was not run. What the prediction read from [rows 5], scalings ahead of the next casts, holds in every trace: in before, e2, e5 and e10 the four scalings stand ahead of three casts and PE waits 4.9 to 6.0 us for the first; in the others casts stand ahead of the scalings, and PE's longest wait at the end of pair 0 is 1.4 us. What turned the order was fewer sevens, or in e11 the sums on POOL; the line in the code did not. Whether seven sevens with the casts forced ahead would do as well was not tried; e11 is the nearest to it, and it takes work off DVE too.
- *The start*, 1.05 + 2.1: mis-sized. At the 67th matmul after is 0.9 us ahead in the profiled execution, and not at all in the mean of six kernels with this start. The first matmul comes 0.87 us later, outside the bounds and past the 6 us that the prediction gave as its own sign of being wrong here, because x, issued after the first weights, is held up by them: 5.59 us from issue to use, 2.95 when it goes first (e3). In the trace of after the weight pieces issued at 0.73, 1.18 and 1.64 land at 4.54, 6.50 and 7.32, and x, issued at 1.17 on the other queue, at 6.67: the pieces of both queues land nearly in the order of their issue. The rest of the term, the clock, went with how long PE stood before that matmul (see the warm-ups). The Trainium skill, "DMA: Bandwidth & Descriptors", section "Issuing engines are not separate DMA queues", said that such DMAs interleave on the same 16 engines; these landings agree. The prediction used it for the upper bound alone and left the lower one above nothing, where it lies below.
- *Sums made later*, -1.0 in pair 1: nothing. The parts cost what was put (the lo part of 384 columns 553 ns, for 0.54 us), but there was room for them. Pair 1 became 1.3 us longer by its window, which is its six matmuls; e8 puts 5 us more on DVE there for 0.1 us.
- *Pair 16 and 17*, 6.1 + 0.3: pairs 15 to 17 take 255.8 us against 260.4 [rows 3, and 82.7 for pair 15], with 12 matmuls more, so 4.6 + 2.7 = 7.3. e7 gives 7.6. The step into pair 17 had the same work in the same order, yet 0.9 of it came there; why stays open.
- *The tail*, 0.3: -0.4. The prediction saw the delay of the first half's scaling (2.07 us after the last matmul in place of 0.5) but took it for smaller than the gain; e4 measures it.

The sum by these: -6.8 + 15.5 + 0.9 + 0 + 7.3 - 0.4 = 16.5 us, the difference of the spans. Of the rivals, the one in which the sevens stay late and the one in which weights wait behind the made-up loads are excluded by the list of waits, the one in which all waits go came nearest, and the start took back what it would have won. For the first of them DVE came close: from 60 to 80 us it is busy 19.97 of 20 us in after, and yet PE waits for nothing there.
